# A two-block network on one core: softmax mixer turned two pairs behind, linear mixer's heads overlapped, context norms fed in piecewise

## The chip, the cores and the metric

The kernel runs on one core of one Trainium2 chip. The metric is the device time of one execution in microseconds (us), the median of several runs. The engines are named as in the profile: PE is TensorE's matmul, PEld its weight load, DVE is VectorE, ACT is ScalarE, POOL is GpSimd, SP is SyncE. Line numbers (L1706) are lines of the kernel before.

## The reference

256 tokens of width 1024 pass through two networks of two blocks each. The first one carries a second stream, 256 context tokens, through its first block: a short convolution, then a SwiGLU FFN, both streams with the same weights; its second block is attention (the tokens attend to themselves and to the context) and an FFN of the tokens alone. The second network has in each block an FFN, a mixer and an FFN; the mixer of its first block is linear (mLSTM, 4 heads), that of its second a sliding-window softmax of 16 heads with 2 key heads and a sink for each head; both have 4 further heads that read a memory. Cut to what the change touches:

```python
def _rms_norm(x, g):
    y = x * lax.rsqrt(jnp.mean(x * x, axis=-1, keepdims=True) + EPS)
    return y * g
# first network, block i
x = x + g2 * _swiglu(_modulate(_rms_norm(x, norm_ffn[i]), sh2, sc2), ffn_w_in[i], ffn_w_out[i])
if update_ctx:
    ctx = ctx + g2c * _swiglu(_modulate(_rms_norm(ctx, norm_ffn[i]), sh2c, sc2c),
                              ffn_w_in[i], ffn_w_out[i])
# linear mixer, one chunk of one head
s = jnp.einsum('bhjd,bhsd->bhjs', qc, kc) * jnp.exp(log_d - m_t[..., None])
num = jnp.einsum('bhjs,bhsv->bhjv', s, vc) + ...
h = num / jnp.maximum(jnp.abs(den), jnp.exp(-m_t))[..., None]
# softmax mixer, one block of 128 queries
m = jnp.maximum(jnp.max(s, axis=-1, keepdims=True), sink)
p = jnp.exp(s - m)
denom = jnp.sum(p, axis=-1, keepdims=True) + jnp.exp(sink - m)
return jnp.einsum('bhgqk,bkhd->bqhgd', p / denom, vn)
```

## The kernel before

Every large product is fp32 split into a high and a low part. `mm3` (L252 to L254) issues three matmuls for one block: high by high, high by low, low by high. Weights stream in by DMA (`wraw`); ACT rounds them to `whi` (L107) and DVE takes the rest as `wlo` (L108). Products go to PSUM banks: in the mixers four main ones (`pm`) for the projections and four auxiliary ones (`pa`) for everything short.

The stages follow one another in one program. By the trace they lie so (us of the span): convolution to 221, FFN of both streams to 597, attention to 810, two FFNs to 1180, linear mixer to 1315, two FFNs to 1693, softmax mixer to 1804, last FFN to the end. An FFN of the tokens alone (`ffn_pairs`) runs a 512-column matmul with the high and low activations side by side (L339) and a 256-column one (L341); its result has two halves in one bank, which `evac` adds to X in two DVE instructions (L1307 and L1376).

Three things set the order. A list scheduler places the instructions by priorities taken from program order. In the mixers `weave(main, side, ratio)` takes steps of two generators in turn: the projections and partial output products as `main` (the filler), the heads as `side`; each `yield` of the heads carries a cost. And `net.between` is a list of small pieces: `mm3` runs one of them after its three matmuls, `flush` runs all that are left.

The names that the change touches. *Norms of the first network*: `row_stats` issues the mean-of-squares matmuls (L414), the reciprocal root (`newton`, L293 to L302) and a matmul that turns the root into rows (L431) as soon as it is called; `modulate` (L584 on) then makes the normed activations `xh`, `xl`. *Linear mixer* (`mixer_a`): for each head the scores with the decay (from L1661), the values, a chain of ten small DVE instructions on `hst` (L1688 to L1697), the normed output `y` (L1700), and its four transposes (L1706), in this order. *Softmax mixer* (`mixer_b`): pairs of heads; `scores(pair)` issues the products (L1895), the masked row maxima (L1900), the exponentials on ACT (L1910) from `lg` into new tiles `ex`, the scaling by the reciprocal sum (L1918 on ACT, L1920 on DVE); `turn(pair, e)` transposes the probabilities (L1927) and splits them to `pth`, `ptl`; `values(pair)` multiplies. Step s runs scores(s), turn(s-1), values(s-2). `lg` and `ex` come from one pool of 8 tiles (`tmp`), the small statistics `bst` from a pool with 2 buffers.

Of the kernel before, what the change touches and what calls it, by code (L numbers as in the profile page):

```python
# [8 lines left out]
F32 = mybir.dt.float32  # L9
# [3 lines left out]
ALU = mybir.AluOpType  # L13
# [3 lines left out]
P = 128  # L17
D = 1024
KB = D // P
T = 256  # L20
# [143 lines left out]
class Net:  # L164
# [241 lines left out]
    def rstd_between(self, accs, ntile, tag):  # L406
# [15 lines left out]
        return r  # L422

    def rows_from_cols(self, r, ntile):

        nc = self.nc
        dg = self.tmp()
        for t in range(ntile):
            nc.vector.tensor_scalar(dg[:, t * P : (t + 1) * P], self.ident, r[:, t : t + 1], None, ALU.mult)
        ps = self.aux_bank()  # L430
        nc.tensor.matmul(ps[:, : ntile * P], self.ones, dg[:, : ntile * P], start=True, stop=True)  # L431
        return ps
# [186 lines left out]
    def ffn(self, xh, xl, sh, sl, parts, evac, between):  # L619
# [5 lines left out]
        for part, (b0, b1) in enumerate(parts):  # L625
            for g in range(b0 // 2, b1 // 2):
                gate = [self.main_bank() for _ in range(2)]
                up = [self.main_bank() for _ in range(2)]
                if first:
                    units = [self.ws.take() for _ in range(4)]  # L630
                    for v in range(2):
                        vs = slice(v * T, (v + 1) * T)
                        for i, dst in enumerate((gate, up)):
                            for h in range(2):
                                self.wstat_unit(units[2 * i + h], [d[:, vs] for d in dst], xh[:, :, vs], xl[:, :, vs], k8, 4 * h)
                else:
                    self.wstat(gate, xh, xl, k8)
                    between("hid", g, 0)
                    self.wstat(up, xh, xl, k8)
# [193 lines left out]
def conv_block(net):  # L833
# [155 lines left out]
    with tc.tile_pool(name="hid0", bufs=1) as hp, tc.tile_pool(name="ada", bufs=2) as net.adap:  # L989
# [28 lines left out]
        for v in range(2):  # L1018
            for g in range(2, 4):
                conv_out(g, (v,))  # L1020
                if v == 0 and g == 2:
                    net.ada_flush()
                    for half in range(2):
                        net.mod_scale(0, 1, half)
            net.modulate(0, 1, v, both[v], net.row_stats(accs[v]), k8, xh[:, :, vsl[v]], xl[:, :, vsl[v]])
        conv_pool.close()
        state = {}

        def evac(part, j, c, ps, v):
            kb = 2 * j + c  # L1030
            for i in range(2) if v is None else (v,):
                net.gated_add(0, 5, kb, i, both[i], ps[:, vsl[i]] if v is None else ps)
                if part == len(FFN0_PARTS) - 1:
                    state[i] = net.block_squares(both[i], kb, state.get(i, []))
                    if kb == KB - 1:
                        if i == 0:
                            net.ada_flush()
                            for half in range(2):
                                net.mod_scale(1, 0, half)
                        net.modulate(1, 0, i, both[i], net.row_stats(state[i]), k8, *(x[:, :, vsl[i]] for x in net.xa))  # L1040

# [73 lines left out]
def attention_block(net):  # L1115
# [6 lines left out]
    with ExitStack() as es:  # L1122
# [20 lines left out]
        def project(q4):  # L1143
# [26 lines left out]
            else:  # L1170
                kb.append(net.main_bank())
            yield from net.xstat_steps(kb[1], (2, 3), xh, xl, ku)
            kr = head_rstd(net, kb, 8, 64, "kr")
# [128 lines left out]
    with tc.tile_pool(name="hid1", bufs=1, reuse_waits="tile") as hp:  # L1302
# [3 lines left out]
        def evac(kb, ps):  # L1306
            for i in range(2):  # L1307
                net.gated_add(1, 5, kb, 0, net.X, ps[:, i, :])
# [55 lines left out]
def ffn2(net, x2, acc, gain, first, last=False, rope=False):  # L1364
# [4 lines left out]
    with tc.tile_pool(name="hid", bufs=1) as hp:  # L1369
# [3 lines left out]
        def evac(kb, ps):  # L1373
            x = net.X[:, kb, :]
            for i in range(2):
                nc.vector.scalar_tensor_tensor(x, ps[:, i, :], 0.5, x, ALU.mult, ALU.add)  # L1376
# [141 lines left out]
def mixer_a(net, x2, acc, gain):  # L1518
# [4 lines left out]
    with tc.tile_pool(name="mixa", bufs=1) as mp:  # L1523
# [74 lines left out]
        with tc.tile_pool(name="mixm", bufs=1) as mm:  # L1598
# [50 lines left out]
            def heads():  # L1649
# [4 lines left out]
                tri = net.k("tri_st")  # L1654
                for h in range(4):
                    while h not in flags:
                        yield WAIT
                    Gc, em, og = env["Gc"], env["em"], env["og", h]
                    vh, vl = vts[h % 2]
                    bc = net.aux_bank()  # L1660
# [16 lines left out]
                    net.split(sdh, sdl, sd[:, : 3 * P])  # L1677
                    yield 0.9
                    hps = [net.aux_bank()[:, : T + 2] for _ in range(2)]
# [17 lines left out]
                    nc.vector.tensor_tensor(st[:, 12:14], st[:, 10:12], st[:, 6:8], ALU.mult)  # L1697
                    y = net.tmp()
                    for t in range(2):
                        nc.vector.scalar_tensor_tensor(y[:, t * T : (t + 1) * T], hps[t][:, :T], st[:, 12 + t : 13 + t],  # L1700
                                                       og[:, t, :], ALU.mult, ALU.mult)
                    yield 1.0
                    pt = net.aux_bank()
# [4 lines left out]
                    for c in range(2):  # L1708
                        b = 2 * h + c
                        net.split(yh[:, b, :], yl[:, b, :], pt[:, c * T : (c + 1) * T], hg[:, b : b + 1])  # L1710
                        done.add(b)
                    yield 0.4

# [49 lines left out]
def mixer_b(net, x2, acc, gain):  # L1763
# [3 lines left out]
    with tc.tile_pool(name="mixb", bufs=1) as mp:  # L1767
# [52 lines left out]
        with tc.tile_pool(name="mixm", bufs=1) as mm:  # L1820
# [56 lines left out]
            def heads():  # L1877
# [6 lines left out]
                def scores(pair):  # L1884
# [5 lines left out]
                    for t in range(2):  # L1890
                        qs = slice(t * P, (t + 1) * P)
                        for i, (q, k) in enumerate(((qh, kh), (qh, kl), (ql, kh))):
                            for e in range(2):
                                rs = slice(64 * e, 64 * e + 64)
                                nc.tensor.matmul(banks[e][:, cols[t]], q[rs, pr, qs], k[rs, gk, : (t + 1) * P], start=i == 0, stop=i == 2)  # L1895
                    st = net.small(24, "bst")
                    lg = [net.tmp() for _ in range(2)]
# [7 lines left out]
                    nc.vector.tensor_tensor(v(2), v(1), sk, ALU.add)  # L1905
                    ex = [net.tmp() for _ in range(2)]
                    for t in range(2):
# [32 lines left out]

                for step in range(10):
                    if step < 8:
# [5 lines left out]
                        yield 1.2  # L1948
                    if 1 <= step < 9:
                        for e in range(2):  # L1950
                            turn(step - 1, e)
                            yield 0.35
                    if step >= 2:
                        values(step - 2)
                        yield 1.3
# [154 lines left out]
```

## Time and profile before

| | us |
|---|---|
| runs shown | 2003.06, 2001.25, 2003.57 (median 2003.06) |
| profiled execution, own time | 2001.8 |
| its span | 2000.0 |
| PE busy | 1982.2 (99%) |
| PE weight load busy | 1764.3 (88%) |
| DVE busy | 1476.4 (74%) |
| ACT busy | 1040.8 (52%) |

The profile is of one execution; 1.8 us of its time lie outside the span. The granted TensorE clock is 1.00 in every slice. A matmul's listed duration is modelled and overlaps the next one, so how fast matmuls follow one another is read from their start times, and an idle PE from a start that comes later than that pace. "Idle before" counts only the part of such a gap in which no matmul is listed as running, so it is shorter than the gap in the starts.

### The profile page before, as it was taken

What the parts mean: (1) busy time and instruction counts of PE and PEld (TensorE: products, weight loads), DVE (VectorE), ACT (ScalarE), POOL (GpSimd) and SP (SyncE); (2) the same over time, 40 slices, a digit from 0 to 9 for tenths busy, and PEclk for the clock granted to TensorE, in tenths of its full rate; (3) what the DMA queues carried; (4) which work ended last, traced back from release to release, by engine and by line L of the source; (5) the groups of instructions that cost most, each with busy time, mean ns of one, the idle gap of its engine ahead of it and who ended that gap; (6) DMA issues with size and microseconds to landing.
All of it is one profiled execution on the core that took longest, in us unless ns stands there. A gap on an engine that the chain in (4) does not pass through costs nothing.

```text
span 2000.0 us, 32108 instructions
## 1 busy us (share of the span) xinstructions
PE 1982.2 (99%) x12478; PEld 1764.3 (88%) x12478; DVE 1476.4 (74%) x2440; ACT 1040.8 (52%) x1752; POOL 5.1 (0%) x26
## 2 busy tenths in 40 slices
PE   9999999999999999999999999999999999999999
PEld 7888988888899999988888899998888888989888
DVE  6988777767477779766587667787767776888774
ACT  5533632123365657655455556655545555676552
POOL 0000000000000000000000000000000000000000
PEclk9999999999999999999999999999999999999999
DMA  8665465667364343566666664556656656525654
GB/s 262 223 200 174 121 190 168 198 234 245 118 185 132 91 122 122 174 191 187 187 195 186 188 183 137 158 179 192 185 187 196 190 180 190 157 76 170 190 179 136
DMA packets 321321, 348.84 MB, mean 174 GB/s; under 512 B 12624, under 2 KB 309712, under 8 KB 321168
## 3 DMA queue, kind: packets, MB, share of 16 engines
q1 hardware_dynamic: 321168, 346.78, 56.4%
q8 instruction: 98, 1.61, 0.3%
q14 instruction: 55, 0.45, 0.1%
HBM read 345.68 MB, written 1.05 MB: 173 GB/s over the span
## 4 chain that ended last, share of the span: by engine, by line
PE 90%; DVE 5%; ACT 3%; issue 1%; DMA 1%; SPq 0%; DVEq 0%; ACTq 0%
PE pg L339 18%; PE pm L252 12%; PE pm L254 12%; PE pm L253 12%; PE po L339 10%; PE pg L341 9%; PE po L341 5%; PE pg L350 2%; DVE wlo L108 1%; PE pa L252 1%; PE pa L253 1%; PE pa L254 1%; PE pg L352 1%; ACT whi L107 1%; PE pa L532 1%
## 5 line engine op out<-in xcount | busy, mean ns | idle before, releaser
L108 DVE TENSOR_TENSOR wlo<-wraw,whi 128x512 fp32r<-128x512 f32 (+1 forms) x785 | 706.2, 916 | 345.4 <-ACT whi L107 338.9
L107 ACT CAST whi<-wraw 128x512 fp32r<-128x512 f32 (+1 forms) x785 | 612.2, 803 | 656.9 <-issue 184.7
L339 PE MATMUL pg<-x,whi 128*128 128x512 f32 x1280 | 346.9, 393 | 0.0
L339 PE MATMUL po<-s,whi 128*128 128x512 f32 x880 | 241.8, 393 | 0.0
L339 PEld LDWEIGHTS pg<-x,whi 128*128 128x128 f32 x1280 | 217.4, 188 | 27.4
L252 PE MATMUL pm<-xh,whi 128*128 128x512 f32 (+1 forms) x576 | 218.3, 380 | 0.7 <-ACT xh L266 0.7
L254 PE MATMUL pm<-xh,wlo 128*128 128x512 f32 (+1 forms) x576 | 218.0, 378 | 0.0
L253 PE MATMUL pm<-xl,whi 128*128 128x512 f32 (+1 forms) x576 | 217.9, 378 | 0.0
L341 PEld LDWEIGHTS pg<-x,wlo 128*128 128x128 f32 x1280 | 194.1, 188 | 26.8
L341 PE MATMUL pg<-x,wlo 128*128 128x256 f32 x1280 | 199.9, 278 | 0.0
L525 DVE SCALAR_TENSOR_TENSOR ada_acc<-wraw,sil,ada_acc 128x1024 f32<-128x1024 f32 x112 | 141.3, 1283 | 37.7 <-DMA wraw<-in_w_ada 36.8
L339 PEld LDWEIGHTS po<-s,whi 128*128 128x128 f32 x880 | 148.1, 188 | 17.2
L341 PEld LDWEIGHTS po<-s,wlo 128*128 128x128 f32 x880 | 136.4, 188 | 20.2
L341 PE MATMUL po<-s,wlo 128*128 128x256 f32 x880 | 140.9, 278 | 0.0
L252 PEld LDWEIGHTS pm<-xh,whi 128*128 128x128 f32 x576 | 108.4, 188 | 20.8 <-ACT xh L266 1.0
L253 PEld LDWEIGHTS pm<-xl,whi 128*128 128x128 f32 x576 | 108.4, 188 | 20.1 <-DVE xl L267 0.4
L254 PEld LDWEIGHTS pm<-xh,wlo 128*128 128x128 f32 x576 | 108.4, 188 | 19.7
L252 PE MATMUL pm<-sh,whi 128*128 128x256 f32 (+1 forms) x352 | 113.5, 322 | 0.0
L254 PE MATMUL pm<-sh,wlo 128*128 128x256 f32 (+1 forms) x352 | 113.2, 322 | 0.0
L253 PE MATMUL pm<-sl,whi 128*128 128x256 f32 (+1 forms) x352 | 112.7, 320 | 0.0
L254 PE MATMUL pm<-whi,xl 128*128 128x256 f32 x368 | 102.9, 280 | 0.0
L252 PE MATMUL pm<-whi,xh 128*128 128x256 f32 x304 | 86.8, 285 | 0.0
(450 smaller groups left out, 3481.6 us busy)
## 6 DMA issues: line engine op xcount, KB each, us to landing
wraw<-in_ffn_w_in SPq DMA_DIRECT2D x264, 512.0 KB, 3.8
wraw<-in_ffn_w_out SPq DMA_DIRECT2D x128, 512.0 KB, 3.6
wraw<-in_w_ada SPq DMA_DIRECT2D x96, 512.0 KB, 4.7
wraw<-in_a_w_in SPq DMA_DIRECT2D x28, 512.0 KB, 3.7
wraw<-in_attn_w_qkv SPq DMA_DIRECT2D x24, 512.0 KB, 3.9
wraw<-in_conv_w_in SPq DMA_DIRECT2D x18, 512.0 KB, 4.7
wraw<-in_ffn_w_out SPq DMA_DIRECT2D x28, 256.0 KB, 2.8
wraw<-in_b_w_in SPq DMA_DIRECT2D x14, 512.0 KB, 3.9
```

The costliest lines, as they stand in the source:

```text
L107: self.nc.scalar.copy(hi[:, cs], raw[:, cs])
L108: self.nc.vector.tensor_tensor(lo[:, cs], raw[:, cs], hi[:, cs].bitcast(F32), ALU.subtract)
L252: mm(ps, ah, bh, start=first, stop=False)
L253: mm(ps, ah, bl, start=False, stop=False)
L254: mm(ps, al, bh, start=False, stop=last)
L339: self.nc.tensor.matmul(pss[c], hi[:, kk, cs], x2[:, done + kk], start=done + kk == 0, stop=False)
L341: self.nc.tensor.matmul(pss[c][:, 0, :], lo[:, kk, cs], x2[:, done + kk, 0, :], start=False, stop=done + kk == nblocks - 1)
L350: mm(ps, hi[:, kk, cs], x2[:, kb], start=kb == 0, stop=False)
L352: mm(ps[:, 0, :], lo[:, kk, cs], x2[:, kb, 0, :], start=False, stop=kb == nblocks - 1)
L525: nc.vector.scalar_tensor_tensor(accs[v], w, c, accs[v], ALU.mult, ALU.add)
L532: nc.tensor.transpose(pt[:, b * P : (b + 1) * P], accs[v][:, (4 * h + b) * P : (4 * h + b + 1) * P], self.ident)
```

## The change

Context norms: where the context stream's norm was computed at once, `norm_between` puts its pieces on the `between` list: five empty ones, four mean matmuls, the root, eight empty ones, and a last piece with the row matmul and `modulate`. This is done for the norm ahead of the first FFN and for the one at its end. `flush` is called before the context half of the FFN's first group, and in the attention's projection before its context part.

Linear mixer: the body of a head is cut into `scores`, `values` and `turn`, and the loop runs scores(h), turn(h-1), values(h).

Softmax mixer: exponentials are written over the logits (`ex = lg`), `bst` gets 4 buffers, and step s runs scores(s), turn(s-2), values(s-3), in 11 steps.

Two evacuations add the second half of the bank first.

```diff
+    def norm_between(self, accs, layer, which, v, src, xh, xl, last=None):
+        env = {}
+        def part(t, i):
+            if not env:
+                env["ps"] = self.aux_bank()
+            ts = slice(t * P, (t + 1) * P)
+            self.nc.tensor.matmul(env["ps"][:, ts], accs[i][:, ts], self.mean, start=i == 0, stop=i == len(accs) - 1)
+        def root():
+            m = self.small(4, "rc_m")
+            r = env["r"] = self.small(4, "rcol")
+            self.nc.vector.tensor_scalar(m[:, :2], env["ps"][:, : 2 * P : P], EPS, None, ALU.add)
+            self.newton(r[:, :2], m[:, :2], "rc")
+        def rest():
+            R = self.rows_from_cols(env["r"], 2)[:, :T]
+            self.modulate(layer, which, v, src, R, list(range(KB)), xh, xl)
+            if last is not None:
+                last()
+        none = [lambda: None]
+        self.between += none * 5 + [partial(part, t, i) for t in range(2) for i in range(len(accs))] + [root] + none * 8 + [rest]
...
+                        if v == 1:
+                            self.flush()
...
+                net.norm_between(accs[v], 0, 1, v, both[v], *parts, conv_pool.close)
...
+                            net.norm_between(state[i], 1, 0, i, both[i], *parts)
...
+            net.flush()
             yield from net.xstat_steps(kb[1], (2, 3), xh, xl, ku)
...
-            for i in range(2):
+            for i in (1, 0):
                 net.gated_add(1, 5, kb, 0, net.X, ps[:, i, :])
...
-            for i in range(2):
+            for i in (1, 0):
                 nc.vector.scalar_tensor_tensor(x, ps[:, i, :], 0.5, x, ALU.mult, ALU.add)
...
+                for h in range(5):
+                    if h < 4:
+                        while h not in flags:
+                            yield WAIT
+                        scores(h)
+                        yield 0.9
+                    if h > 0:
+                        turn(h - 1)
+                        yield 0.4
+                    if h < 4:
+                        values(h)
+                        yield 1.0
...
-                    st = net.small(24, "bst")
+                    st = net.sp.tile([P, 24], F32, name="bst", tag="bst", bufs=4)
...
-                    ex = [net.tmp() for _ in range(2)]
+                    ex = lg
...
-                for step in range(10):
+                for step in range(11):
...
-                    if 1 <= step < 9:
+                    if 2 <= step < 10:
                         for e in range(2):
-                            turn(step - 1, e)
+                            turn(step - 2, e)
                             yield 0.35
-                    if step >= 2:
-                        values(step - 2)
+                    if step >= 3:
+                        values(step - 3)
                         yield 1.3
```

How this moves PE's instructions, at three places.

PE, start of the attention's projection (`pm<-whi,xh` is a projection of the token stream, L414 and, in the changed kernel, L432 the mean matmuls of the context norm). Before:

```order
L252 MATMUL pm<-whi,xh 128x256
L253 MATMUL pm<-wlo,xh 128x256
L414 MATMUL pa<-mean,acc_5420 128x128
L414 MATMUL pa<-mean,t 128x128
L414 MATMUL pa<-mean,acc_5420 128x128
L414 MATMUL pa<-mean,t 128x128
L254 MATMUL pm<-whi,xl 128x256
```

In the changed kernel:

```order
L254 MATMUL pm<-whi,xl 128x256
L432 MATMUL pa<-mean,acc_5425 128x128
L252 MATMUL pm<-whi,xh 128x256
L253 MATMUL pm<-wlo,xh 128x256
L254 MATMUL pm<-whi,xl 128x256
L432 MATMUL pa<-mean,t 128x128
L252 MATMUL pm<-whi,xh 128x256
```

The four mean matmuls stood together behind 8 projection matmuls; they now stand one by one, the first behind 18. The row matmul (L431, L456 in the changed kernel) follows the last mean matmul after 57 projection matmuls, where it was 15.

PE, linear mixer, around the transposes of head 1 (before; L1706) and of head 0 (changed; L1747; L1695 is L1661 of before, the rows with `qkh` and `qkl` are the scores of head 1). Before:

```order
L254 MATMUL pm<-x_10242,wlo 128x256
L252 MATMUL pm<-x_10242,whi 128x256
L1706 MATMUL pa<-kc,t 128x128 x2
L253 MATMUL pm<-x_10242,whi 128x256
L1706 MATMUL pa<-kc,t 128x128 x2
L254 MATMUL pm<-x_10242,wlo 128x256
```

In the changed kernel:

```order
L1695 MATMUL pa<-rb,sel 128x256
L252 MATMUL pa<-qkh 128x256
L253 MATMUL pa<-qkl,qkh 128x256
L254 MATMUL pa<-qkh,qkl 128x256
L252 MATMUL pa<-qkh 128x128
L253 MATMUL pa<-qkl,qkh 128x128
L254 MATMUL pa<-qkh,qkl 128x128
L1747 MATMUL pa<-kc,t 128x128 x4
```

The transposes of a head moved behind the next head's scores and stand together; the last head's still stand two by two behind filler.

PE, softmax mixer (L1895 and, in the changed kernel, L1949 are the products of `scores`; L1927 and L1981 the transposes of `turn`). Before, scores of pair 2 with the turn of pair 1:

```order
L1895 MATMUL pa<-kh,bq_17372 128x128 x2
L1895 MATMUL pa<-kl,bq_17372 128x128 x2
L1895 MATMUL pa<-kh,bq_17373 128x128 x2
L1895 MATMUL pa<-kh,bq_17372 128x256 x2
L1895 MATMUL pa<-kl,bq_17372 128x256 x2
L1895 MATMUL pa<-kh,bq_17373 128x256 x2
L1927 MATMUL pa<-kc,t 128x128 x6
```

In the changed kernel, scores of pair 4 with the turn of pair 2:

```order
L254 MATMUL pm<-yh,wlo 128x256
L1949 MATMUL pa<-kh,bq_17379 128x128 x2
L1949 MATMUL pa<-kl,bq_17379 128x128 x2
L1949 MATMUL pa<-kh,bq_17380 128x128 x2
L1949 MATMUL pa<-kh,bq_17379 128x256 x2
L1949 MATMUL pa<-kl,bq_17379 128x256 x2
L1949 MATMUL pa<-kh,bq_17380 128x256 x2
L1981 MATMUL pa<-kc,t 128x128 x6
```

The turn that stands behind scores(s) is now that of pair s-2. The number of matmuls is the same in both programs; DVE has 7 instructions more and ACT 2 fewer, all in the root ahead of the first FFN, where the form without logarithms is taken.

In SBUF the two further `bst` buffers (96 bytes each in a partition) move every tile of the left-hand pools that are opened later by 192 bytes: the weight tiles `wraw`, `whi`, `wlo` among them. Tiles of the right-hand pools, such as the activations `x2` of `ffn_pairs` and the mixers, stay where they were.

## Rows read from the trace of the kernel before

**Rows 1.** The page: span, busy time of each engine, and a group of matmuls of the FFNs (listed busy time and mean are modelled; the last column is idle time before).

```profile
span 2000.0 us, 32108 instructions
PE 1982.2 (99%) x12478; PEld 1764.3 (88%) x12478; DVE 1476.4 (74%) x2440; ACT 1040.8 (52%) x1752; POOL 5.1 (0%) x26
L341 PE MATMUL pg<-x,wlo 128*128 128x256 f32 x1280 | 199.9, 278 | 0.0
```

**Rows 2.** Busy time in stretches of 50 us; columns: stretch, its length, PE, PEld, DVE, ACT, POOL busy (instructions), granted clock, DMA share, GB/s.

```profile
600.00:650.00 50.00, 49.83 (x414) 47.29 (x412) 36.04 (x86) 29.49 (x65) 0.31 (x1) 1.00 0.43 132
1200.00:1250.00 50.00, 49.35 (x417) 47.62 (x415) 38.61 (x107) 34.04 (x87) 0.00 (x0) 1.00 0.49 137
1750.00:1800.00 50.00, 46.21 (x390) 42.05 (x391) 41.55 (x163) 38.13 (x126) 0.00 (x0) 1.00 0.25 76
```

**Rows 3.** What PE waited for, by line: waiting line, releasing line, us in total, times, longest.

```profile
PE pa L1927 <- ACT t L1918: 1.5, 3, 0.6
...
PE pa L1706 <- DVE t L1700: 1.3, 3, 0.6
PE pa L414 <- DVE acc L615: 1.3, 3, 0.8
...
PE pa L1859 <- DVE t L1816: 1.1, 1, 1.1
PE pa L1895 <- DVE ptl L267: 0.9, 1, 0.9
...
PE pa L431 <- DVE t L429: 0.3, 2, 0.2
```

**Rows 4.** Timeline of PE and DVE at the start of the attention's projection; columns: start, us, engine, line, operation, count, idle before and its releaser.

```profile
597.98 0.28 PE L253 MATMUL pm<-wlo,xh 128*128 128x256 f32 x1
599.10 0.46 PE L414 MATMUL pa<-mean,acc 128*128 128x128 f32 x2 [0.84 <-DVE acc L615]
...
598.53 0.42 DVE L615 TENSOR_TENSOR acc<-acc,t 128x256 f32<-128x256 f32 x1
...
602.86 1.95 DVE L593 TENSOR_TENSOR t<-C,pa 128x256 f32<-128x256 f32 x4 [0.85 <-PE pa L431]
...
610.13 0.68 DVE L267 TENSOR_TENSOR xl<-t,xh 128x512 fp32r<-128x512 f32 x1
```

**Rows 5.** Timeline of PE and DVE in the linear mixer, at the transposes of head 0.

```profile
1246.60 0.28 PE L252 MATMUL pm<-whi,x 128*128 128x256 f32 x1
1247.43 0.41 PE L1706 MATMUL pa<-kc,t 128*128 128x128 f32 x2 [0.55 <-DVE t L1700]
...
1241.92 0.16 DVE L1689 SCALAR_TENSOR_TENSOR hst<-hst 128x2 f32<-128x2 f32 x1
...
1246.81 0.87 DVE L1700 SCALAR_TENSOR_TENSOR t<-pa,hst,og 128x256 f32<-128x256 f32 x2
```

**Rows 6.** Timeline of PE in the softmax mixer, two places: a turn behind its scores, and scores that wait for a bank.

```profile
1758.42 0.28 PE L1895 MATMUL pa<-kh,bq 64*128 64x256 f32 x2
1759.34 0.87 PE L1927 MATMUL pa<-kc,t 128*128 128x128 f32 x5 [0.64 <-ACT t L1918]
...
1773.11 0.27 PE L1895 MATMUL pa<-kh,bq 64*128 64x128 f32 x1
1774.32 0.39 PE L1895 MATMUL pa<-kh,bq 64*128 64x128 f32 x2 [0.94 <-DVE ptl L267]
```

**Rows 7.** Busy time in stretches of 5 us of the softmax mixer, columns as in rows 2.

```profile
1750.00:1755.00 5.00, 4.78 (x40) 4.46 (x41) 5.00 (x28) 3.17 (x11) 0.00 (x0) 1.00 0.06 20
1755.00:1760.00 5.00, 4.34 (x40) 3.56 (x39) 4.58 (x19) 5.00 (x18) 0.00 (x0) 1.00 0.25 58
1760.00:1765.00 5.00, 4.74 (x42) 4.12 (x41) 4.66 (x22) 4.44 (x16) 0.00 (x0) 1.00 0.24 66
1765.00:1770.00 5.00, 5.00 (x47) 4.58 (x47) 4.97 (x21) 4.63 (x16) 0.00 (x0) 1.00 0.32 104
...
1775.00:1780.00 5.00, 4.41 (x38) 3.75 (x36) 3.61 (x15) 3.38 (x13) 0.00 (x0) 1.00 0.32 105
```

**Rows 8.** Timeline of PE, DVE and SP's queue at the end of the span.

```profile
1995.39 0.62 PE L339 MATMUL po<-s,whi 128*128 128x512 f32 x2
1995.59 1.67 DVE L1376 SCALAR_TENSOR_TENSOR X<-po,X 128x256 f32<-128x256 f32 x4 [8.10 <-PE po L341]
...
1995.86 0.39 PE L341 MATMUL po<-s,wlo 128*128 128x256 f32 x2
1996.51 1.12 SPq L1378 DMA_DIRECT2D outT<-X  x2
```

**Rows 9.** Timeline of PE, three runs of 256-column matmuls, the first and the last row of each: 15 steps of the first FFN (moving operand `xh`), 9 steps of the linear mixer's start (moving `x2`), 17 steps later in that mixer (moving `whi`).

```profile
221.48 0.28 PE L253 MATMUL pm<-xl,whi 128*128 128x256 f32 x1
...
223.28 0.28 PE L253 MATMUL pm<-xl,whi 128*128 128x256 f32 x1
...
1186.88 0.28 PE L252 MATMUL pm<-x,whi 128*128 128x256 f32 x1
...
1187.94 0.28 PE L252 MATMUL pm<-x,whi 128*128 128x256 f32 x1
...
1270.03 0.28 PE L252 MATMUL pm<-whi,x 128*128 128x256 f32 x1
...
1271.95 0.28 PE L254 MATMUL pm<-whi,x 128*128 128x256 f32 x1
```

More of the change, by code (lines that the diff above doesn't have):

```diff
@@ L1024, in conv_block @@
                         net.mod_scale(0, 1, half)
-            net.modulate(0, 1, v, both[v], net.row_stats(accs[v]), k8, xh[:, :, vsl[v]], xl[:, :, vsl[v]])
-        conv_pool.close()
+            parts = (xh[:, :, vsl[v]], xl[:, :, vsl[v]])
+            if v == 0:
+                net.modulate(0, 1, v, both[v], net.row_stats(accs[v]), k8, *parts)
+            else:
+                net.norm_between(accs[v], 0, 1, v, both[v], *parts, conv_pool.close)
         state = {}
@@ L1039, in evac @@
                                 net.mod_scale(1, 0, half)
-                        net.modulate(1, 0, i, both[i], net.row_stats(state[i]), k8, *(x[:, :, vsl[i]] for x in net.xa))
+                        parts = [x[:, :, vsl[i]] for x in net.xa]
+                        if i == 0:
+                            net.modulate(1, 0, i, both[i], net.row_stats(state[i]), k8, *parts)
+                        else:
+                            net.norm_between(state[i], 1, 0, i, both[i], *parts)
         net.ffn(xh, xl, sh, sl, FFN0_PARTS, evac, net.ada_at)
@@ L1654, in heads, with scores @@
                 tri = net.k("tri_st")
[L1655 to L1659, printed above, removed]
+                sds, ys = {}, {}
+                def scores(h):
+                    Gc = env["Gc"]
                     bc = net.aux_bank()
@@ L1677, in heads, with values @@
                     net.split(sdh, sdl, sd[:, : 3 * P])
-                    yield 0.9
+                    sds[h] = sdh, sdl
+                def values(h):
+                    em, og = env["em"], env["og", h]
+                    vh, vl = vts[h % 2]
+                    sdh, sdl = sds.pop(h)
                     hps = [net.aux_bank()[:, : T + 2] for _ in range(2)]
@@ L1697, in heads @@
                     nc.vector.tensor_tensor(st[:, 12:14], st[:, 10:12], st[:, 6:8], ALU.mult)
-                    y = net.tmp()
+                    y = ys[h] = net.tmp()
                     for t in range(2):
@@ L1701, in heads, with turn @@
                                                        og[:, t, :], ALU.mult, ALU.mult)
-                    yield 1.0
+                def turn(h):
+                    y = ys.pop(h)
                     pt = net.aux_bank()
@@ L1711, in heads @@
                         done.add(b)
-                    yield 0.4
+                for h in range(5):
[10 more added lines that the diff above has]
+                        yield 1.0
             weave(chain(project(), mixer_partials(net, MIX_A[:-1], yh, yl, done)), heads(), RATIO_A)
```

## The prediction, made before the changed kernel ran

> **What bounds the kernel now.** I read the page first: PE is busy 1982.2 of 2000.0 us, and no other engine comes near it [rows 1]. The reader is to see there that the whole kernel has 18 us in which PE could be idle, so a change that leaves the matmuls as they are can win a few us at most, unless it changes how fast they follow one another. The second view is the busy time by stretches: the softmax mixer holds the largest hole, 50.00 - 46.21 = 3.8 us of PE in 1750 to 1800, the linear mixer 0.65 in 1200 to 1250, the start of the attention 0.17 from 600 on [rows 2]. The third is what PE waited for, line by line; it names the lines that the change moves: L1927, L1706, L414, L431 [rows 3]. Last come the timelines at those lines [rows 4 to 6], which show how long the starts of two matmuls lie apart. A listed wait is shorter than that: at 1758.42 the next start comes 0.92 us later, 0.80 over the pace of 0.12, where 0.64 is listed, so 0.16 is to be added to each listed wait [rows 6]; at 1246.60 it is 0.83 - 0.12 = 0.71 against 0.55, 0.16 again [rows 5].
>
> **The change part by part,** summed against the profiled execution's own 2001.8 us (span 2000.0 and 1.8 around it); the median of the runs is 2003.06, so 1.3 is added at the end.
>
> *Norm at the attention's start.* From 597.98 to the first mean matmul at 599.10 are 1.12 us, 1.00 over the pace: DVE delivers `acc` only at 598.53 + 0.42 = 598.95 [rows 4]. In the changed order the first mean matmul stands behind 18 projection matmuls, not 8: ten more at 0.12 are 1.2 us, so it comes at about 599.2, after `acc`. The 1.00 goes. The row matmul's listed 0.3 is two waits, the longest 0.2 [rows 3]; the one here, about 0.15 and 0.16 with the pace, goes too, since 57 matmuls (6.7 us) now cover the root: another 0.3. Against this four mean matmuls now interrupt the pace singly; 0 to 4 x 0.16, taken 0.2. Sum -1.1. What is late next is `modulate`: it ran from 602.86 to 610.13 + 0.68 = 610.8, eight us [rows 4], and now starts about 6 us later and ends at about 616.5. By the order the context's projection wants its first blocks at about 615.7 and its last at about 617.8 (matmuls counted at 0.12), so it is just in time; DVE has room, 36.0 of 50 us busy in 600 to 650 [rows 2]. If it isn't, up to 2 us come back. Bounds -1.4 to +1.
>
> *Norm ahead of the first FFN.* Before, its mean matmuls already stood among FFN matmuls, and no wait is listed there but the other of L431's two [rows 3]. The root takes ten small DVE instructions instead of two on ACT and three on DVE; one costs 0.16 [rows 5], so about 1 us more, beside the token half of the first group that PE works on meanwhile. Taken 0, between -0.3 and +1.6 (all ten bare).
>
> *Linear mixer.* The three listed waits of the transposes for `y` are 1.3 us, with 0.16 each 1.8 [rows 3, 5]. The chain behind them goes from 1241.92 to 1246.81 + 0.87 [rows 5], some 5.8 us, and now has the rest of a head and the next head's scores as cover. All three go; the last head's turn has no scores behind it and stays. Transposes that stand together interrupt the filler once, not twice: 0.1. What the moved turn delays is `yh`, `yl` of a head, by about one head; the partial products that read them are later filler, and DVE has 38.6 of 50 us busy here [rows 2], so I cost it at nothing; without that cover a filler group would wait at most what the turns waited. Sum -1.9, bounds -2.3 to +0.5.
>
> *Softmax mixer.* The three waits of L1927 for the scaled exponentials, 1.5 + 3 x 0.16 = 2.0 [rows 3, 6], go, since the turn now takes a pair whose exponentials are one step older. Scores that waited for a bank (1773.11 to 1774.32, 1.21 - 0.12 = 1.1, released by the split of a turn [rows 6]) use the same ring of four banks after it; I take half, -0.5. The wait of 1.1 at L1859 [rows 3] lies ahead of the heads and stays. Against that stands DVE: busy 5.00 + 4.58 + 4.66 + 4.97 = 19.2 of the 20 us from 1750 to 1770 [rows 7]. Two of the three waits lie there, so of their 1.2 us only 0.8 can be had before DVE is full; and by the order little filler is left between the scores of pairs 5 and 7, about ten matmuls, since the partial product that needs the values of pair 3 comes a step later. Give-back 0.5 taken, 0 to 4.5 possible (the rise of a pair from PE's pace to DVE's over four pairs). Writing the exponentials in place takes no instruction away; it only frees tiles of `tmp`, which hold the logits longer now. Sum -2.0, bounds -4 to +2.
>
> *Evacuation order.* The four adds of the last two blocks take 1.67 us from 1995.59 [rows 8]. In both programs the first add of a bank waits for the last matmul into that bank and the second for the first, whichever half it is. So 0; if halves counted separately, one add, 1.67 / 4 = 0.4, would start earlier: -0.4 at the very end.
>
> The Trainium skill ("PSUM — Partial Sum Buffer", PSUM bank collisions raise a hardware error) says that two engines in one bank and partition quadrant collide at any address, which is why the wait is for the bank; it speaks against this edit, the sum by it is the same 0, and no run so far shows the halves apart.
>
> *Addresses.* The weight tiles move by 192 bytes, and the trace shows three paces for 256-column matmuls at the same granted clock of 1.00: (223.28 - 221.48) / 15 = 0.120 us, (1187.94 - 1186.88) / 9 = 0.118, (1271.95 - 1270.03) / 17 = 0.113 [rows 9]. Which placement makes which is not shown. The 1280 such matmuls of the FFN pairs [rows 1] and, by the program, about 1000 of the mixers have one operand that moves against the other. Between 0.120 for all (1280 x 0.002 + 1000 x 0.007 = +9.6) and 0.113 for all (1280 x 0.005 = 6.4, and half of the 1000 at 0.005, 2.5: -8.9) I take 0, as both paces stand mixed in the kernel already.
>
> The Trainium skill ("TensorE: Matmul & The Clock Gate", Wait — 56ns, not 53.3ns?) has a fixed step of N / 2.4 GHz plus some 2.5 ns, an estimate of 0.109 us for 256 columns at any address. By that rule the address term is 0 with no bounds; the trace doesn't agree, its paces lie 0.004 to 0.011 above and apart.
>
> Sum: -1.1 + 0 - 1.9 - 2.0 + 0 + 0 = -5.0, so 1996.8 on the profiled execution's scale, 1998.1 beside the median.
>
> **The rivals.** *DVE bounds the softmax mixer.* The 96% of DVE in 1750 to 1770 speak for it, the 3.6 of 5 from 1775 on against it [rows 7]. Its 2.5 come back wholly: -1.1 - 1.9 + 0.5 = -2.5, 2000.6. *More goes than I count.* The whole hole of 3.8 us in that mixer [rows 2] closes, since each stall is fed by the one before it, and the pace falls by a quarter of its bound: -1.1 - 1.9 - 3.8 - 2.2 = -9.0, 1994.1. The fixed waits (L1859) speak against it. *Slower, by the address.* If the shift of the weights against `x2` brings the 0.120 pace of rows 9 to the FFN pairs, their 1280 512-column matmuls take part at twice the price (1280 x 0.004 = +5.1), to +14.7 at most; at two thirds, +10, the sum is +5.0: 2008.1. It decides from +9 on, a mean of 2.5 ns over these 3,560 matmuls. For it speaks that the paces differ at all and that the offset changes by no whole 512 bytes; against it that 0.118 is near the upper end already.
>
> **How the numbers follow.** Forecast 0.58, DVE-bound 0.16, more 0.14, slower 0.12. The predicted time is 1998.1; the likeliest case's own range is 1995 to 2001. What can be told from no change is 0.2%, 4.0 us: faster is below 1999.05. Of the forecast's 0.58 seven tenths, 0.41, lie below that, with the 0.14 that is 0.55; same 0.17 + 0.16 = 0.33; slower 0.12. The range goes from 1991 (the case "more" with another 3 of pace) to 2006 (the DVE case and half of the address term's 9.6 together, 2005.4), leaving out about 0.16.
>
> **What would show it.** In the changed profile no wait of the linear mixer's transposes but the last head's; no L414-like wait at 597 to 600; in 1750 to 1800 PE's hole 1.8 smaller, without a new wait for DVE's masked maxima or for `bst`; the pace of the three runs in rows 9 the same within 1 ns. It is wrong if scores or turns of the softmax mixer wait on DVE for more than 2 us in all, if the context projection waits for `xl` near 616, or if FFN pairs take longer from start to start.

## The result and the profile after

The changed kernel takes 2010.61 us (median of 6 executions, 2007.78 to 2012.34), the kernel before 2003.01 beside it: a ratio of 1.0039, 95% interval 1.003 to 1.0049. It is slower by 7.6 us, where 5.0 less was forecast, and outside the range of 1991 to 2006. The profiled execution has a span of 2008.0, 8.0 more than before, which agrees with the medians.

The page of the changed kernel: span, busy time of the engines, and the two largest groups of matmuls that read `x2`.

```profile
span 2008.0 us, 32117 instructions
PE 1992.8 (99%) x12478; PEld 1775.2 (88%) x12478; DVE 1476.4 (74%) x2447; ACT 1040.3 (52%) x1750; POOL 5.1 (0%) x26
...
L339 PE MATMUL pg<-x,whi 128*128 128x512 f32 x1280 | 348.7, 394 | 0.0
...
L341 PE MATMUL pg<-x,wlo 128*128 128x256 f32 x1280 | 204.4, 282 | 0.0
```

The group of L339 in the kernel before:

```profile
L339 PE MATMUL pg<-x,whi 128*128 128x512 f32 x1280 | 346.9, 393 | 0.0
```

Against [rows 1] PE's busy time has grown by 10.6 us with the same 12478 instructions, and the span by only 8.0. So the idle time has shrunk, as the change means it to, and the matmuls have become slower, some of them by a lower clock (below). The group of L341 went from 199.9 to 204.4 and that of L339 from 346.9 to 348.7; they have no idle time before them, so by the listed times these are some 6 us of the span. Neither the code of these matmuls nor their place in the order was edited.

What PE waited for in the changed kernel (L1747, L1913, L1949, L1981 are L1706, L1859, L1895, L1927 of before):

```profile
PE pa L252 <- DVE bst L1954: 1.8, 2, 1.2
...
PE pa L1913 <- DVE t L1870: 1.1, 1, 1.1
...
PE pa L414 <- DVE acc L640: 0.7, 2, 0.5
...
PE pa L1981 <- DVE yl L267: 0.5, 1, 0.5
...
PE pa L456 <- DVE t L454: 0.4, 2, 0.2
...
PE pa L1981 <- DVE bst L1967: 0.2, 1, 0.2
```

Against [rows 3], L1706's wait for `y` (1.3) has no counterpart left, L414 lost its longest wait, and the wait for the scaled exponentials (1.5) is gone. The row matmul's two waits (L431, now L456) are still there: the one at the attention stands at 607.23 with 0.22 us. In place of the wait for the exponentials stand 1.8 us in which the products of `values` wait for a bank that DVE still reads (`bst`, the masked maxima, L1954); before, this wait was

```profile
PE pa L252 <- DVE bst L1900: 0.3, 1, 0.3
```

The timeline of PE at the paces of [rows 9]: 22 steps with `x2` moving at the linear mixer's start, 21 steps later in that mixer.

```profile
1185.83 0.29 PE L252 MATMUL pm<-x,whi 128*128 128x256 f32 x1
...
1188.47 0.29 PE L253 MATMUL pm<-x,whi 128*128 128x256 f32 x1
...
1268.40 0.28 PE L253 MATMUL pm<-wlo,x 128*128 128x256 f32 x1
...
1270.89 0.29 PE L253 MATMUL pm<-wlo,x 128*128 128x256 f32 x1
```

These are 2.64 / 22 = 0.120 us and 2.49 / 21 = 0.119; they were 0.118 and 0.113. The granted clock is 1.00 at both places, as before.

It is not 1.00 everywhere. Stretches of 5 us in the softmax mixer, columns as in [rows 2]:

```profile
1750.00:1755.00 5.00, 3.92 (x33) 3.52 (x31) 4.86 (x24) 2.14 (x5) 0.00 (x0) 1.00 0.60 194
1755.00:1760.00 5.00, 5.00 (x26) 4.09 (x24) 4.45 (x24) 3.83 (x17) 0.00 (x0) 0.62 0.00 0
1760.00:1765.00 5.00, 5.00 (x32) 4.61 (x33) 3.74 (x16) 3.35 (x14) 0.00 (x0) 0.70 0.27 81
```

From 1755 to 1765 PE is listed as fully busy, yet has 26 and 32 matmuls where the fullest stretch of [rows 7] has 47: the listed busy share does not show that the clock fell. The clock's loss is 5 x 0.38 + 5 x 0.30 = 3.4 us. The timeline there shows what went before, and the pace at either level:

```profile
1752.38 0.28 PE L254 MATMUL pm<-yh,wlo 128*128 128x256 f32 x1
1753.74 0.66 PE L1913 MATMUL pa<-kc,t 128*128 128x128 f32 x4 [1.08 <-DVE t L1870]
...
1760.90 0.41 PE L252 MATMUL pm<-yh,whi 128*128 128x256 f32 x1
...
1762.18 0.41 PE L252 MATMUL pm<-yh,whi 128*128 128x256 f32 x1
...
1763.25 0.28 PE L252 MATMUL pm<-yh,whi 128*128 128x256 f32 x1
...
1763.96 0.28 PE L252 MATMUL pm<-yh,whi 128*128 128x256 f32 x1
```

PE waits for the rotated queries: the start at 1753.74 comes 1.36 us after the one at 1752.38. It runs transposes and the short products of the scores of pairs 1 and 2, and from 1756 on the clock is granted at half, which is 1.2 of 2.4 GHz: six steps of filler take 1.28 us, 0.213 each, and six steps after 1763.25 take 0.71, 0.118 each.

To see where the time went, the start of the n-th matmul in one trace was subtracted from that in the other; the table gives what each stage added (us, against the profile of before).

| stage | changed | addresses only | distance restored | norms and linear |
|---|---|---|---|---|
| start of the span | -0.5 | -0.9 | -0.3 | +1.7 |
| convolution, first FFN | -0.6 | -0.2 | -0.5 | -0.4 |
| attention and its norm | -1.8 | +0.3 | -1.5 | -3.0 |
| FFNs to the linear mixer | +1.6 | +1.6 | +0.2 | 0.0 |
| linear mixer | +0.2 | +1.3 | -1.6 | -1.9 |
| FFNs to the softmax mixer | +3.9 | +3.9 | +0.4 | 0.0 |
| softmax mixer | +3.4 | +1.0 | +2.6 | +0.3 |
| last FFN | +1.8 | +1.8 | +0.2 | 0.0 |
| sum | +8.0 | +8.8 | -0.6 | -3.4 |

The first column is the result: 7.3 us are lost in FFN stages in which no order was changed, and 3.4 in the softmax mixer, which was to bring 2.0. The first row lies ahead of every edit, so it is what two executions differ by; the +1.7 of the last column is a stretch at half clock from 40 to 44 us. The other columns are the first, second and ninth of the experiments that follow.

### The profile page after: what moved, and what is told of

Read it like the earlier page. It is cut to its first block, busy times and chain, and to the rows that moved or that the text cites. A ratio compares the mean times of both kernels' runs of the same rounds, so it can differ in the third digit from the quotient of the medians.

```text
span 2008.0 us, 32117 instructions
## 1 busy us (share of the span) xinstructions
PE 1992.8 (99%) x12478; PEld 1775.2 (88%) x12478; DVE 1476.4 (74%) x2447; ACT 1040.3 (52%) x1750; POOL 5.1 (0%) x26
## 4 chain that ended last, share of the span: by engine, by line
PE 92%; DVE 4%; ACT 3%; issue 1%; DMA 1%; SPq 0%; DVEq 0%; ACTq 0%
PE pg L339 18%; PE pm L252 13%; PE pm L254 13%; PE pm L253 13%; PE po L339 10%; PE pg L341 9%; PE po L341 5%; PE pg L350 2%; DVE wlo L108 1%; PE pa L252 1%; PE pa L253 1%; PE pa L254 1%; PE pg L352 1%; ACT whi L107 1%; PE pa L557 1%
## 5 line engine op out<-in xcount | busy, mean ns | idle before, releaser
L108 DVE TENSOR_TENSOR wlo<-wraw,whi 128x512 fp32r<-128x512 f32 (+1 forms) x785 | 706.2, 916 | 350.7 <-ACT whi L107 344.8
L339 PE MATMUL pg<-x,whi 128*128 128x512 f32 x1280 | 348.7, 394 | 0.0
L339 PEld LDWEIGHTS pg<-x,whi 128*128 128x128 f32 x1280 | 218.8, 188 | 27.7
L339 PE MATMUL po<-s,whi 128*128 128x512 f32 x880 | 241.8, 393 | 0.0
L341 PEld LDWEIGHTS pg<-x,wlo 128*128 128x128 f32 x1280 | 196.6, 188 | 28.0
L341 PE MATMUL pg<-x,wlo 128*128 128x256 f32 x1280 | 204.4, 282 | 0.0
L339 PEld LDWEIGHTS po<-s,whi 128*128 128x128 f32 x880 | 148.1, 188 | 17.2
L341 PEld LDWEIGHTS po<-s,wlo 128*128 128x128 f32 x880 | 136.4, 188 | 20.2
L341 PE MATMUL po<-s,wlo 128*128 128x256 f32 x880 | 140.9, 278 | 0.0
```

The costliest lines, as they stand in the source:

```text
L108: self.nc.vector.tensor_tensor(lo[:, cs], raw[:, cs], hi[:, cs].bitcast(F32), ALU.subtract)
L339: self.nc.tensor.matmul(pss[c], hi[:, kk, cs], x2[:, done + kk], start=done + kk == 0, stop=False)
L341: self.nc.tensor.matmul(pss[c][:, 0, :], lo[:, kk, cs], x2[:, done + kk, 0, :], start=False, stop=done + kk == nblocks - 1)
```

## The experiments

Two causes stood for the 7.3 us in the FFNs: the addresses (the weights moved by 192 bytes against `x2`), or a change in what reaches these stages (the swapped adds, the weight stream). For the softmax mixer: half clock through the scores that stand close together, or DVE. Each time is the median beside that of the kernel before on the same chip.

**The addresses alone.** To the kernel before only this is added, ahead of the weight tiles:

```diff
+    es.enter_context(tc.tile_pool(name="gap", bufs=1)).tile([P, 48], F32, name="gap")
     net.ws = WeightStream(net, es, stream_specs(a), 5, 4, 2)
```

> The kernel before with one unused tile of 192 bytes opened ahead of the weight tiles: the same instructions in the same order, only the addresses of the changed kernel. If the address of the weights against x2 costs the time, the 256-column matmuls of x2 go from a mean step of 0.1156 to about 0.119 us and the 512-column ones from 0.2308 to 0.2326, with the granted clock at 1.00 throughout: 2280 steps of 3.3 ns and 1280 of 1.8 ns are +9.8 us, about 2012.5. If the FFN pairs are slower for the swapped adds or for what the earlier stages do to the weight stream, nothing changes: 2003.

Measured 2011.48 against 2002.13, ratio 1.0046 (1.0032 to 1.006). Its page:

```profile
L339 PE MATMUL pg<-x,whi 128*128 128x512 f32 x1280 | 348.5, 394 | 0.0
...
L341 PE MATMUL pg<-x,wlo 128*128 128x256 f32 x1280 | 204.3, 281 | 0.0
```

These are the figures of the changed kernel. An unused tile of 192 bytes costs 9.3 us, more than the whole change does, and its FFN stages lose in the table what those of the changed kernel lose.

**The distance restored, and two ways with the turns.** All three kernels below are the changed one with the right-hand tiles, `x2` among them, moved by the same 192 bytes; the second also takes back the order of turns and values, the third delays the scores of pair 2:

```diff
-    es.enter_context(tc.tile_pool(name="top", bufs=1, side="right")).tile([P, 104], F32, name="fill3")
+    es.enter_context(tc.tile_pool(name="top", bufs=1, side="right")).tile([P, 56], F32, name="fill3")
...
-                    if 2 <= step < 10:
+                    if 1 <= step < 9:
-                            turn(step - 2, e)
+                            turn(step - 1, e)
...
-                        yield 1.2
+                        yield 4.0 if step == 1 else 1.2
```

> The changed kernel with the right-hand tiles moved by the same 192 bytes (the unused tile fill3 48 columns narrower), so that x2 stands against the weights as before. Address theory: the steps of x2 go back to 0.1156 and 0.2308 us, the time falls by 9 to 10 us to about 2001, and a stretch at half clock near 1756 stays in most executions. If it is the absolute address of a tile that counts and not the distance, s and the weights are still shifted and x2 now as well: the steps stay slow or others get slow, above 2008. If the cause is not in the addresses: 2010.

> As the run before it, but the softmax mixer runs turn(s-1) and values(s-2) as in the kernel before (exponentials still in place, four bst buffers). If the half clock at 1756 to 1763 comes from the scores of three pairs standing close together, the clock stays at 1.00; the waits of L1927 come back (2.0 us) and the stretch of 3.4 us goes: about 1.5 us faster than the realigned kernel, near 1999.5. If the clock falls for the wait ahead of the rotated keys alone, which both kernels have, it falls here as well.

> As the realigned kernel, but the cost of the step behind the scores of pair 1 is 4.0 and not 1.2, so that by the order 21 projection matmuls stand ahead of the scores of pair 2. If close scores make the clock fall, it stays at 1.00 here with the turns two pairs behind: 3.4 us less than the realigned kernel, near 1997.5. If the clock falls all the same, no change.

Measured: distance restored 2001.80, ratio 0.9995 (0.9987 to 1.0004); with the old turns 1999.05, 0.9983 (0.9974 to 0.9991); with the scores of pair 2 delayed 1999.76, 0.9988 (0.9979 to 0.9997). In the first of them the groups of L339 and L341 are back:

```profile
L339 PE MATMUL pg<-x,whi 128*128 128x512 f32 x1280 | 346.7, 393 | 0.0
...
L341 PE MATMUL pg<-x,wlo 128*128 128x256 f32 x1280 | 199.7, 278 | 0.0
```

So it is the place of `x2` relative to the weights that counts, and not the place of either alone: with the weights alone moved it is slow, with both moved it is not. The fourth case is the run at distance 256 further below, in which `x2` lies as here and the weights as before: slow again. Stretches of the softmax mixer, first with the distance restored:

```profile
1750.00:1755.00 5.00, 5.00 (x26) 4.51 (x25) 4.67 (x27) 4.54 (x19) 0.00 (x0) 0.62 0.00 0
1755.00:1760.00 5.00, 5.00 (x36) 4.61 (x35) 3.05 (x15) 3.87 (x14) 0.00 (x0) 0.70 0.31 105
```

with the old turns:

```profile
1745.00:1750.00 5.00, 3.95 (x24) 3.54 (x25) 5.00 (x28) 2.99 (x10) 0.00 (x0) 0.79 0.19 65
1750.00:1755.00 5.00, 5.00 (x40) 4.83 (x39) 3.79 (x15) 3.91 (x16) 0.00 (x0) 0.87 0.00 0
```

and with the scores of pair 2 delayed:

```profile
1745.00:1750.00 5.00, 3.89 (x27) 3.28 (x26) 5.00 (x27) 2.83 (x8) 0.00 (x0) 0.87 0.29 101
1750.00:1755.00 5.00, 5.00 (x41) 4.71 (x39) 3.86 (x16) 4.86 (x19) 0.00 (x0) 0.79 0.00 0
```

By the column of the clock the first loses 3.4 us, the other two 5 x 0.34 = 1.7 each. I had expected the clock to stay up there; it falls for half as long. So the 1999.05 near the expected 1999.5 came about in another way than expected, and the 1997.5 of the last was missed. Over all executions, 9 of 11 with the distance restored have a mean clock of 0.998 or less, 2 of 11 in each of the other two, and 2 of 27 of the kernel before; such a mean doesn't say where in the span the clock fell. That is evidence that scores standing close together make the stretch longer. That they start it is refuted: the clock also falls in traces whose softmax mixer is that of before, here with the swapped adds alone:

```profile
1754.00:1755.00 1.00, 1.00 (x7) 1.00 (x6) 1.00 (x5) 1.00 (x4) 0.00 (x0) 0.50 0.00 0
```

By the few executions there are, nearly all that the order of the turns costs is this clock. The two executions with the distance restored that have a mean clock of 1.00 took 1997.72 and 1998.33 us; the five such with the old turns took 1997.37 to 1998.55.

**Single parts.** The hunks of the diff one group at a time, each on the kernel before; the softmax edits with `x2` moved along.

> Only the two context norms of the change, addresses as before. The matmuls of the changed kernel with the addresses restored run 2.1 us ahead of before from index 3000 to 3500 and 0.4 more from 1000 to 1500; if that is the norms, this kernel is 2.0 to 2.5 us faster than before in every execution, and its lead at the end of the span is the same as behind the attention's start. By the prediction it is 1.1 us.

> Only the linear mixer's new order. By the prediction the waits of the transposes for y go, but the last, 1.9 us less. By the lead that the realigned kernel gains there (1.4 us between index 7500 and 8000) it is nearer 1.3. If the lead is given back in the partial products behind, nothing.

> Only the softmax mixer's edits (exponentials in place, four bst buffers, turns two pairs behind), with x2 at its old distance from the weights. By the prediction 2.0 us less. Half-clock theory: the scores of three pairs stand together, the clock falls for some 6.6 us in most executions and the median is about 1 us slower than before; executions whose mean clock is 1.00 are about as fast as those of before, since the waits for the exponentials are replaced by waits for the maxima (bst).

> Only the swapped order of the two adds of a bank. Both adds wait for the whole bank: no change, 2002, and the last two stores start as long after the last matmul as before. If the halves are independent, the end comes 0.1 to 0.4 us earlier, which the time can't show but the timeline of the end can.

Against 2001.36: norms 2001.01, ratio 0.9998 (0.999 to 1.0007); linear mixer 2000.78, 0.9998 (0.9989 to 1.0007); softmax mixer 2004.01, 1.0013 (1.0005 to 1.0022); evacuation order 2001.89, 1.0003 (0.9994 to 1.0012). One at a time only the softmax edits can be told from nothing, and they cost. The expected 2 us of the norms and 1.3 to 1.9 of the linear mixer are in the traces of these runs (-3.1 and -1.8 in the stages edited; 0.9 of the 3.1 is a change of pace in matmuls that no edit touches, see the end), but not in the times. The clock explains a part: two of the eleven executions with the norms alone had a mean clock of 1.00 where 20 of 33 of the kernel before had, and the profiled one lost 1.5 us in the softmax mixer, where its clock fell. It is not all: the executions at 1.00 have a median of 1999.7 with the norms (two) and 2000.1 with the linear mixer (six), against 2000.6 of the kernel before. So what each part brings alone is read from one trace each and not shown by the times. The softmax edits alone are not explained to the end either: 5 of their 11 executions have a mean clock of 1.00 and still a median of 2003.7, 3.1 us over that 2000.6, where no such cost was seen with the other edits beside them. Part of it, 1.6 us in the profiled one, lies in stages ahead of that mixer.

The swapped adds do nothing, as the end of the two timelines shows; first the changed kernel, then that edit alone:

```profile
2003.80 0.39 PE L341 MATMUL po<-s,wlo 128*128 128x256 f32 x2
2004.45 1.12 SPq L1413 DMA_DIRECT2D outT<-X  x2
```

```profile
1997.35 0.40 PE L341 MATMUL po<-s,wlo 128*128 128x256 f32 x2
1997.99 1.12 SPq L1378 DMA_DIRECT2D outT<-X  x2
```

From the last matmuls to the stores are 0.65 and 0.64 us; in [rows 8] it is 1996.51 - 1995.86 = 0.65.

**Norms and linear mixer together,** with nothing of the softmax mixer, so that no address moves.

> The norms and the linear mixer of the change, nothing of the softmax mixer, so that all addresses are those of before. By the traces of the single parts the norms lead by 2.5 to 3.0 us behind the attention's start and the linear mixer by 1.6: together 4 us, 1998 where before is 2002. If single parts give their lead back in a stage behind (each of them alone measured within 0.1% of before), 2001.

Measured 1998.26 against 2001.88, ratio 0.9982 (0.9973 to 0.9991): 3.6 us faster than the kernel before, as expected, and level with the restored kernel with the old turns (0.9983), the two fastest here. Its waits keep the one that the softmax edits were made for, and have none of L1747:

```profile
PE pa L1981 <- ACT t L1972: 1.6, 3, 0.6
```

In its trace the clock stays at 1.00 in the softmax mixer and falls near the start of the span instead, in the convolution, behind a wait of 1.54 us for weights that ends at 38.82: from 40 to 45 us it is 0.66 in the mean, which costs 5 x 0.34 = 1.7 us.

**Which distances.** The kernel before with only the width of the unused right-hand tile `fill3` changed, so that `x2` and the other right-hand tiles start elsewhere; distances are modulo 512 bytes, by the program's layout, since the traces list no addresses. Of the right-hand tiles the groups of L339 and L341 read `x2` alone.

```diff
-    es.enter_context(tc.tile_pool(name="top", bufs=1, side="right")).tile([P, 104], F32, name="fill3")
+    es.enter_context(tc.tile_pool(name="top", bufs=1, side="right")).tile([P, 120], F32, name="fill3")
```

> The kernel before with only the right-hand tiles moved so that x2 starts at the weights' own place modulo 512 bytes (64 in the kernel before, 384 in the changed one). Address theory: the distance modulo 512 sets the step of the matmuls that read both. At distance 0 the first FFN shows 0.227 us for 512 columns against 0.2308, and 0.1177 for 256 columns against 0.1156: in the FFN pairs that is 1280 x (-0.0038 + 0.0021) = -2 us, in the mixers about +2, so 2002 in all. Rival: 64 is the only good place, and every other costs the 9 us of 384: 2011.

> As the run before it, with x2 at 128 bytes. No run shows this distance. Address theory: a step of its own, between 0.113 and 0.119 us for 256 columns; steps of other tiles (s, and the normed activations of the attention's FFN) stay at 0.1156 and 0.2308. Rival as before: 2011.

> As the two before it, with x2 at 256 bytes. Between 2000 and 2012; the steps of 256 and 512 columns give the time: each 0.001 us of them is 2.3 and 1.3 us.

> x2 at 320 bytes (64 and 256) from the weights modulo 512, nothing else changed. If the pattern repeats with 128 or 256 bytes: steps of 0.1156 and 0.2308 us as at 64, time 2002. If 64 alone is good: 0.1186 and 0.233, 2011.

> x2 at 192 bytes (64 and 128). If every odd multiple of 64 is good: 2002. If the pattern repeats with 256 bytes only, it can be slow: 2011.

> x2 at 32 bytes. If only multiples of 128 are bad: 0.1156 and 0.2308 us or better, 2002 or less. If it must be an odd multiple of 64: slow, up to 2011; half way gives half, 2006.

> x2 at 96 bytes; as for 32 bytes. If 32 and 96 differ, the pattern is not mirrored about 64.

| distance in bytes | 0 | 32 | 64 | 96 | 128 | 192 | 256 | 320 | 384 |
|---|---|---|---|---|---|---|---|---|---|
| against before, us | +10.3 | +6.7 | 0 | +11.6 | +9.6 | +1.7 | +10.4 | 0.0 | +9.3 |
| group of L339 (512 columns), us | 349.4 | 350.1 | 346.9 | 350.1 | 350.7 | 349.0 | 349.4 | 346.7 | 348.5 |
| group of L341 (256 columns), us | 203.6 | 200.8 | 199.9 | 205.9 | 203.0 | 198.7 | 203.6 | 199.7 | 204.3 |

The entry at 64 is the kernel before itself, the one at 384 the run with the addresses alone. Two distances, 64 and 320, are good in both groups. By its time 192 can't be told from 64 (ratio 1.0006, 0.9994 to 1.0017), but its trace is not the same: the 512-column matmuls are as slow as at 0, the 256-column ones the fastest of all, and its FFN stages add up to +2.0. So "every odd multiple of 64 is good" is not shown. 0 and 256 agree in both groups, and so do 64 and 320, as a repeat with 256 bytes would have it; 128 and 384 don't quite, and there it was the weights that moved. 32 and 96 differ by 5.1 us in the group of L341, so the pattern is not mirrored about 64. My mean of 2002 for distance 0, from the pace of other tiles in the first FFN, was wrong, and so was the rival that 64 alone is good. Lines of L339 and L341 of the pages, at 0, at 192 and at 320:

```profile
L339 PE MATMUL pg<-x,whi 128*128 128x512 f32 x1280 | 349.4, 394 | 0.0
...
L341 PE MATMUL pg<-x,wlo 128*128 128x256 f32 x1280 | 203.6, 281 | 0.0
```

```profile
L339 PE MATMUL pg<-x,whi 128*128 128x512 f32 x1280 | 349.0, 394 | 0.0
...
L341 PE MATMUL pg<-x,wlo 128*128 128x256 f32 x1280 | 198.7, 277 | 0.0
```

```profile
L339 PE MATMUL pg<-x,whi 128*128 128x512 f32 x1280 | 346.7, 393 | 0.0
...
L341 PE MATMUL pg<-x,wlo 128*128 128x256 f32 x1280 | 199.7, 278 | 0.0
```

## Why the prediction was wrong

*Addresses: the step that failed.* "Between 0.120 for all [...] and 0.113 for all [...] I take 0, as both paces stand mixed in the kernel already." Measured alone the term is +9.3, close to its upper bound of 9.6. That both paces stood mixed was no reason for the middle: 0.113 and 0.118 are not two placements. In the kernel before, 256-column matmuls with `x2` in the second network run at either pace in stretches of twelve steps and rarely between, all at the one distance; with the addresses alone moved no such stretch is below 0.116. So the kernel before stood at the good end, and a move could lose much and win little. The rows at 0.120 in [rows 9] belong to other tiles (`xh` and `xl` moving), which kept that pace: 0.119 in the changed kernel. The kernel has unused tiles, fill1 and fill3 to fill8, ahead of its buffers; they could have been read as a sign that the distance was chosen. The rival "slower, by the address", with 2008.1 and a chance of 0.12, was the right mechanism, and the prediction named the sign of it: FFN pairs that take longer from start to start. Its split was off (3.5 ns for each 256-column matmul and 1.4 for each 512-column one of the FFN pairs, from the page's 204.4 - 199.9 and 348.7 - 346.9 over 1280, not twice as much for the longer).

*Softmax mixer: wrong.* Forecast -2.0; +2.6 in the trace with the distance restored, with the clock's 3.4 in it. The waits for the exponentials went, as said. But waits for banks held by the masked maxima, 1.8 us where 0.3 were, came in their place, near to what the DVE rival had, and the clock fell to half for some 7 us, a loss of 3.4, which no term or rival had. With the distance restored, going back to the old turns makes the median 2.75 us lower (2001.80 to 1999.05); at a mean clock of 1.00 the two orders can't be told apart (two and five executions), so no gain of the turns shows there either.

*Norms: right in sign, one wait wrong.* Against the forecast -1.1 the trace gains 2.1 at the attention's start, but about 0.5 of it is a stretch of the projection at 0.113 and not 0.118 us a step, which also shows in the runs with the addresses alone and the linear mixer alone, whose norms are those of before. The wait of 1.00 is gone, and `modulate` came in time: no wait for `xl` near 616. The row matmul's wait did not go, though the prediction counted it as covered by 57 matmuls: 0.22 us at 607.23, 0.15 before. The norm ahead of the first FFN, forecast 0, brought 0.4 in every trace with it.

*Linear mixer: right.* Forecast -1.9; -1.6 to -2.1 in the traces with the distance at its old value. In the changed kernel the slower matmuls take it back: +1.3 in the column of the addresses alone, +0.2 in all.

*Evacuation order: right.* 0.

The sum without addresses and softmax mixer was -3.0; the kernel with just that measures -3.6 (-1.8 to -5.4). So of the 12.6 us between -5.0 and +7.6, some 9 are the addresses and some 4 to 5 the softmax mixer, with about 1 the other way from the norms.

## What to carry to other kernels

An edit that changes only the number or size of a small buffer moves every tile opened behind it, and the pace of later matmuls may hang on where two operands lie towards each other: compare the addresses as well as the order, and compare the time per instruction of groups that weren't touched before looking for waits. When a busy engine's count of instructions falls in a stretch, look at the granted clock there first. Measure parts of a bundle together as well as alone: here the two useful parts could not be told from nothing one at a time, showed together, and were hidden in the whole by one harmful part and by 192 bytes.

## What was not expected of the hardware

The step of back-to-back fp32 matmuls depended on the distance between moving and stationary operand in SBUF: at 64 and 320 bytes the 1280 pairs of the FFN stages took 346.9 + 199.9 and 346.7 + 199.7 us, at 0 and 256 349.4 + 203.6, at 192 349.0 + 198.7, all at a granted clock of 1.00 in these stages. Other matmuls of the same two lines, which read the left-hand `s` and so kept their distance, kept their time; the line is the same before and in the changed kernel:

```profile
L341 PE MATMUL po<-s,wlo 128*128 128x256 f32 x880 | 140.9, 278 | 0.0
```

Why a distance sets the pace is not shown.

The address is not all of the pace. Runs of 256-column matmuls stood at 0.113 or at 0.118 us for a whole stretch, from one trace to the next, with nothing edited there: 198 steps of the first FFN's last group (`sh` moving, `whi` held) took 0.1178 us each in the kernel before and 0.1133 with the norms alone, with norms and linear mixer, and at distance 320, at a clock of 1.00. This is worth 0.9 us, and it is what the -3.0 of the last column of the table has over the -2.1 of the norms. What picks the pace is open.

The Trainium skill ("TensorE: Matmul & The Clock Gate", Wait — 56ns, not 53.3ns?) gives one fixed step for a warm clock; the traces here don't agree: 256 columns took 0.113, 0.118 and 0.120 us by place.

While matmuls ran, PE's clock fell to half for 3 to 10 us in 14 of the 18 traces: in 11 of them 2 to 4 us behind the wait of 1.1 us for the rotated queries, in three at 40 us in the convolution. The other four show no such fall, though PE waits for the queries there as well. What starts it in one execution and not in the next stays open, and so does the rest of what the softmax edits cost alone.
